# A 256 KB store of zeros on the ACT queue, beside the first loads of a fused multiply and GELU

## The chip, the cores and the metric

One core of a Trainium2 chip runs the kernel alone. The metric is the device time of one execution in microseconds (us), median of several runs.

## The reference

```python
# x, y: 1024 x 4096 float32
z = x * y
return 0.5 * z * (1 + tanh(sqrt(2 / pi) * (z + 0.044715 * z ** 3)))
```

Two inputs of 16.8 MB are read and one output of 16.8 MB is written: 50.33 MB.

## The kernel before

Each of the 128 partitions holds 32768 elements of x in SBUF. They are overwritten in place by the product and then by its GELU. The y values come in three pieces through a ring of half that size. SP issues all loads and stores, and the first two of them stand ahead of the program's first barrier ("hoisted").

```python
X_LOADS = [(0, 16384), (16384, 32768)]
Y_LOADS = [(0, 16384, 0), (16384, 24576, 0), (24576, 32768, 8192)]
STEP = 4096
STORES = [(0, 16384), (16384, 32768)]
# ...
_hoist(nc, [load_x(0).ins, load_y(0).ins])
load_x(1)
for i in (1, 2):
    nc.sync.wait_ge(sem_mul, (Y_LOADS[i][1] - Y_LOADS[1][0]) // STEP)
    load_y(i)

n = 0
for i, (a, b, r) in enumerate(Y_LOADS):
    # ... DVE waits for the x load and the y load concerned
    for c in range(a, b, STEP):
        nc.vector.tensor_mul(out=xs[:, c : c + STEP], in0=xs[:, c : c + STEP],
                             in1=ys[:, r + c - a : r + c - a + STEP]).then_inc(sem_mul, 1)
        n += 1
        nc.scalar.wait_ge(sem_mul, n)
        nc.scalar.activation(out=xs[:, c : c + STEP], in_=xs[:, c : c + STEP],
                             func=GELU).then_inc(sem_act, 1)

for i, (a, b) in enumerate(STORES):
    nc.sync.wait_ge(sem_act, b // STEP)
    nc.sync.dma_start(out=out_r[:, a:b], in_=xs[:, a:b]).then_inc(sem_o[i], 16)
# ... SP waits for both stores
```

So the one SP queue carries, in this order: x (8.4 MB), y (8.4 MB), x (8.4 MB), y (4.2 MB), y (4.2 MB), a store (8.4 MB), a store (8.4 MB).

Of the kernel before, what the change touches and what calls it, by code (L numbers as in the profile page):

```python
# [1 line left out]

# [4 lines left out]


F32 = mybir.dt.float32
GELU = mybir.ActivationFunctionType.Gelu_apprx_tanh  # L10
# [7 lines that stand above are left out]
Y_RING = 16384  # L18


def _hoist(nc, issued):

    here = nc.cur_bb.bb.instructions
    first = nc.main_func.blocks[0].instructions
    for ins in issued:
        del here[next(k for k, i in enumerate(here) if i is ins or i.name == ins.name)]
    engine = issued[0].engine
    at = next(
        k
        for k, i in enumerate(first)  # L30
        if i.engine == engine and type(i).__name__ == "InstDrain"
    )
    first[at:at] = issued


@with_exitstack
def kernel(
    ctx: ExitStack,
    tc: tile.TileContext,
    x: bass.AP,  # L40
    y: bass.AP,
    out: bass.AP,
):
    nc = tc.nc
    P = nc.NUM_PARTITIONS

    x_r = x.flatten_outer_dims().rearrange("(p a) c -> p (a c)", p=P)
    y_r = y.flatten_outer_dims().rearrange("(p a) c -> p (a c)", p=P)
    out_r = out.flatten_outer_dims().rearrange("(p a) c -> p (a c)", p=P)
    total_f = x_r.shape[1]  # L50


    tc.close()
    tc.compile()  # L54

    xs = nc.alloc_sbuf_tensor("xs", [P, total_f], F32).ap()
    ys = nc.alloc_sbuf_tensor("ys", [P, Y_RING], F32).ap()
    sem_x = [nc.alloc_semaphore(f"sem_x{i}") for i in range(len(X_LOADS))]
    sem_y = [nc.alloc_semaphore(f"sem_y{i}") for i in range(len(Y_LOADS))]
    sem_o = [nc.alloc_semaphore(f"sem_o{i}") for i in range(len(STORES))]  # L60
    sem_mul = nc.alloc_semaphore("sem_mul")
    sem_act = nc.alloc_semaphore("sem_act")

    def load_x(i):
        a, b = X_LOADS[i]
        return nc.sync.dma_start(out=xs[:, a:b], in_=x_r[:, a:b]).then_inc(sem_x[i], 16)  # L66

    def load_y(i):
        a, b, r = Y_LOADS[i]
        return nc.sync.dma_start(  # L70
            out=ys[:, r : r + b - a], in_=y_r[:, a:b]
        ).then_inc(sem_y[i], 16)

    _hoist(nc, [load_x(0).ins, load_y(0).ins])
    load_x(1)
    for i in (1, 2):
        nc.sync.wait_ge(sem_mul, (Y_LOADS[i][1] - Y_LOADS[1][0]) // STEP)
        load_y(i)

    n = 0  # L80
    for i, (a, b, r) in enumerate(Y_LOADS):
        for j, (xa, xb) in enumerate(X_LOADS):
            if xa <= a < xb:
                nc.vector.wait_ge(sem_x[j], 16)
        nc.vector.wait_ge(sem_y[i], 16)  # L85
        for c in range(a, b, STEP):
            nc.vector.tensor_mul(  # L87
                out=xs[:, c : c + STEP],
                in0=xs[:, c : c + STEP],
                in1=ys[:, r + c - a : r + c - a + STEP],  # L90
            ).then_inc(sem_mul, 1)
            n += 1
            nc.scalar.wait_ge(sem_mul, n)
            nc.scalar.activation(  # L94
                out=xs[:, c : c + STEP], in_=xs[:, c : c + STEP], func=GELU
            ).then_inc(sem_act, 1)

    for i, (a, b) in enumerate(STORES):
        nc.sync.wait_ge(sem_act, b // STEP)
        nc.sync.dma_start(out=out_r[:, a:b], in_=xs[:, a:b]).then_inc(sem_o[i], 16)  # L100
    for i in range(len(STORES)):
        nc.sync.wait_ge(sem_o[i], 16)
    nums = sorted(s.num for s in [*sem_x, *sem_y, *sem_o, sem_mul, sem_act])
    assert nums == list(range(nums[0], nums[-1] + 1))
    nc.sync.sem_clear(range(nums[0], nums[-1] + 1))


# [1 line left out]
_INS = ['x', 'y']  # L109
_OUTS = [((1024, 4096), 'float32')]  # L110


# [23 lines left out]
```

## Time and profile before

| what | value |
|---|---|
| time, median of 3 runs | 121.02 us (120.82 to 121.17) |
| span of the profiled run | 119.5 us |
| DVE, ACT busy | 29%, 25% |
| packets of the one DMA queue, share of 16 engines | 98.5% |
| bytes read and written | 33.55 + 16.78 MB |

A "packet" in the profile is one record of a transfer on one of the 16 DMA engines. Here each one with data has the size of one partition's row: 64 KB, or 32 KB for the two short y pieces. The records don't name the engine; they were strung together by their times. In the trace of before they string into 16 rows of 63 packets (56 with data), which run side by side: the first packet of each starts between 1.01 and 1.70 us, and together they fill 98.5% of 16 times the span. So a delay of "0.7 us per engine" on all 16 is 0.7 us of the kernel.

These are the two lines of the timeline in which DVE starts on the second and on the third y piece (start, duration, instruction, idle time before and what ended it):

```profile
70.47 8.76 DVE L87 TENSOR_TENSOR xs<-xs,ys 128x4096 f32<-128x4096 f32 x2 [11.70 <-DMA ys<-in_y_dram]
...
80.88 8.76 DVE L87 TENSOR_TENSOR xs<-xs,ys 128x4096 f32<-128x4096 f32 x2 [1.66 <-DMA ys<-in_y_dram]
```

DVE starts 0.09 us after the third piece has landed (80.79 and 80.88 us in the chain of waits), and as soon after the second, so the third landed 10.41 us after the second. For 4.19 MB at the rate of the other stretches (432 to 435 GB/s, worked out in the prediction) 9.7 us would do.

### The profile page before, as it was taken

To read this page: it belongs to the slowest core of one execution; us is meant where nothing else is said; L and a number is where in the kernel's file an instruction comes from. 1 tells how busy PE (TensorE), PEld (TensorE's weight loads), DVE (VectorE), ACT (ScalarE), POOL (GpSimd) and SP (SyncE) were. 2 spreads that over 40 slices of the span, in tenths; PEclk is the share of its full clock that TensorE was granted. 3 is DMA by queue.
4 is the path that set the end of the run, shared out by engine and by line. 5 is a ranking of instruction groups with operands and counts; after the bars stand their busy time and mean duration, and the time that the engine had idled before them with its cause. 6 is when DMAs were issued, how large, how long until landed. Compare 5 with 4: busy or idle time off the path is not lost.

```text
span 119.5 us, 68 instructions
## 1 busy us (share of the span) xinstructions
DVE 35.0 (29%) x8; ACT 30.2 (25%) x9; POOL 0.2 (0%) x4
## 2 busy tenths in 40 slices
DVE  0000000000000199999600049959990000000000
ACT  3000000000000006797780000977479200000000
POOL 0000000000000000000000000000000000000000
DMA  9889888998899889988898989998899888988890
GB/s 351 351 373 680 351 351 351 636 417 351 351 636 417 351 351 526 526 351 351 351 526 351 504 373 482 395 526 351 351 395 658 351 351 351 702 351 351 351 680 22
DMA packets 1008, 50.33 MB, mean 421 GB/s; under 512 B 112, under 2 KB 112, under 8 KB 112
## 3 DMA queue, kind: packets, MB, share of 16 engines
q1 hardware_dynamic: 1008, 50.33, 98.5%
HBM read 33.55 MB, written 16.78 MB: 421 GB/s over the span
## 4 chain that ended last, share of the span: by engine, by line
DMA 53%; DVE 22%; ACT 3%; SPq 0%; issue 0%; DVEq 0%
DMA ys<-in_y_dram 53%; DVE xs L87 22%; ACT xs L94 3%; SPq L66 0%; DVEq L85 0%
## 5 line engine op out<-in xcount | busy, mean ns | idle before, releaser
L87 DVE TENSOR_TENSOR xs<-xs,ys 128x4096 f32<-128x4096 f32 x8 | 35.0, 4421 | 54.7 <-DMA ys<-in_y_dram 54.7
L94 ACT ACTIVATE xs<-xs 128x4096 f32<-128x4096 f32 x8 | 28.9, 3617 | 61.1 <-DVE xs L87 61.1
L94 ACT ACT_TABLE_LOAD x1 | 1.3, 1283 | 1.9 <-PEq L54 1.9
L120 POOL MEMSET const-bfloat16-1.0<- 128x1 bf16 x1 | 0.1, 102 | 0.0
L120 POOL MEMSET const-uint8-127<- 128x1 uint8 x1 | 0.1, 102 | 0.0
L120 POOL MEMSET const-float32-1.0<- 128x1 f32 x1 | 0.1, 99 | 0.0
L120 POOL MEMSET const-float32-0.0<- 128x1 f32 x1 | 0.1, 98 | 0.2 <-issue 0.2
## 6 DMA issues: line engine op xcount, KB each, us to landing
ys<-in_y_dram SPq DMA_DIRECT2D x2, 4096.0 KB, 21.1
xs<-in_x_dram SPq DMA_DIRECT2D x2, 40.3
out_dram<-xs SPq DMA_DIRECT2D x2, 31.9
ys<-in_y_dram SPq DMA_DIRECT2D x1, 40.8
```

What stands on the lines that cost most here:

```text
L87: nc.vector.tensor_mul(out=xs[:, c : c + STEP], in0=xs[:, c : c + STEP], in1=ys[:, r + c - a : r + c - a + STEP],).then_inc(sem_mul, 1)
L94: nc.scalar.activation(out=xs[:, c : c + STEP], in_=xs[:, c : c + STEP], func=GELU).then_inc(sem_act, 1)
L120: nc = _bacc.Bacc("TRN2", target_bir_lowering=False, num_devices=1)
```

## The change

Its intent can be read from the name of the scratch tensor, "first_write": let some harmless write to DRAM be the first one of the execution. DVE fills a small tile with zeros. ACT stores it, each row four times, to a scratch tensor that nobody reads. Both stand ahead of the first barrier. The counts of the multiply semaphore shift by one, because the memset uses the same semaphore.

```diff
+    ws = nc.alloc_sbuf_tensor("ws", [P, 128], F32).ap()
+    sem_w = nc.alloc_semaphore("sem_w")
...
+    scratch = nc.dram_tensor("first_write", [P, 4, 128], F32, kind="Internal").ap()
+    fill = nc.vector.memset(ws[:, :], 0.0).then_inc(sem_mul, 1)
+    ready = nc.scalar.wait_ge(sem_mul, 1)
+    first = nc.scalar.dma_start(out=scratch, in_=ws.unsqueeze(1).to_broadcast([P, 4, 128]))
+    first.then_inc(sem_w, 16)
+    _hoist(nc, [fill.ins])
+    _hoist(nc, [ready.ins, first.ins])
     _hoist(nc, [load_x(0).ins, load_y(0).ins])
...
-        nc.sync.wait_ge(sem_mul, (Y_LOADS[i][1] - Y_LOADS[1][0]) // STEP)
+        nc.sync.wait_ge(sem_mul, 1 + (Y_LOADS[i][1] - Y_LOADS[1][0]) // STEP)
...
-    n = 0
+    n = 1
...
+    nc.sync.wait_ge(sem_w, 16)      # at the end, beside the waits for the stores
```

More of the change, by code (lines that the diff above doesn't have):

```diff
@@ L102 @@
         nc.sync.wait_ge(sem_o[i], 16)
-    nums = sorted(s.num for s in [*sem_x, *sem_y, *sem_o, sem_mul, sem_act])
+    nc.sync.wait_ge(sem_w, 16)
+    nums = sorted(s.num for s in [*sem_x, *sem_y, *sem_o, sem_w, sem_mul, sem_act])
     assert nums == list(range(nums[0], nums[-1] + 1))
```

## The prediction

> **What bounds the kernel now.** I read the page from the top: busy shares, the slices with the DMA row, the queue's share, then the chain of waits.
>
> ```profile
> span 119.5 us, 68 instructions
> DVE 35.0 (29%) x8; ACT 30.2 (25%) x9; POOL 0.2 (0%) x4
> ...
> DMA packets 1008, 50.33 MB, mean 421 GB/s; under 512 B 112, under 2 KB 112, under 8 KB 112
> ...
> q1 hardware_dynamic: 1008, 50.33, 98.5%
> ```
>
> No compute engine is busy for a third of the span, while the packets of the one DMA queue took 98.5% of what 16 engines have. The queue carries 50.33 MB in 112 tiny packets (seven DMAs times 16 engines: the semaphore writes) and 896 large ones. The trace's packet records give the durations: a 64 KB packet takes 2.42 us, a 32 KB one 1.21 us, nearly all alike. Each engine moves 50.33 MB / 16 = 3.146 MB, the equal of 48 packets of 64 KB, so 48 x 2.42 = 116.2 us of the 119.5 are plain transfer.
>
> The chain of waits in order of time seems to tell another story:
>
> ```profile
> 0.44 40.80 DMA ys<-in_y_dram
> ...
> 41.34 17.44 DVE xs L87 x4
> 58.78 0.02 issue
> 58.80 21.99 DMA ys<-in_y_dram
> ...
> 80.88 8.77 DVE xs L87 x2
> ...
> 89.68 3.62 ACT xs L94
> ```
>
> It runs through four multiplications and ends at 93.3 us with the last activation; the last store then takes until 119.4. This is a chain of dependences, not of resources: behind each piece the DMA queue must also be non-empty. It always is. The y pieces are issued at 50.13 and 58.80, while the second x load lands only near 60; the first store is issued at 62.45, when two y pieces are still queued (the second lands at 80.8); the second store is issued at 93.3, and the first lands at 62.45 + 37.7 = 100.15. So the slack of the issues is about 10, 18 and 7 us. What sets the end is the number of bytes and the dead times of the DMA engines.
>
> Where are these dead times? I cut the span at the landings (41.24, 70.40, 80.82, 100.15, end 119.43) and divided the bytes of each piece by its time. The last store has 8.39 MB in 19.28 us, 435 GB/s; the first store 8.39 in 19.33, 434; the second x load with the first y piece 12.58 in 29.13, 432. Two stretches are slower. The first two loads, 16.78 MB, need 38.6 us at 435 GB/s and land at 41.24: 2.7 us of start, of which 1.0 is the time until the first packet and some 0.65 the first packet of each engine (2.6 to 3.3 us instead of 2.42). And the last y piece takes 10.42 us for 4.19 MB, 402 GB/s, where 9.7 would do: 0.7 us lost. In the packet records its last two packets per engine take about 1.8 and 1.35 us instead of 1.21, and they are those just before the first store to HBM. No such loss comes before the second store, nor between any two loads. So the first write to HBM of the execution costs about 0.7 us of all engines' time. This is what the change can aim at: a small early store would pay that cost at a time when the engines wait for their first data anyway.
>
> [...]
>
> **The change part by part.**
>
> 1. A memset of 128 x 128 on DVE before the first barrier. DVE is otherwise idle until 41.3 us. By width, against the 4421 ns of a 4096-wide multiplication, it is some 0.15 to 0.3 us (my estimate). It lies beside the issue of the first loads, on another engine: 0 on the path.
>
> 2. ACT waits for it and issues the store; such an issue keeps a sequencer 0.33 to 0.43 us here. So ACT would reach the first barrier at about 0.3 + 0.4 = 0.7 to 1.0 us, and SP itself gets there only at about 0.9, after its two issues. The barriers may move by some 0.2 us, and with them only the issue of the second x load (1.93 us, needed by the engines at 40) and the activation table load (1.28 us, needed at 45.8). Off the path: 0. The first load is issued at 0.00 by SP and needs nothing from DVE or ACT.
>
> 3. The store's bytes: 262,144 B / 16 = 16 KB for each engine; at 64 KB in 2.42 us, 0.60 us. This is on the path, since the engines have no idle time later.
>
> 4. Its packets. The source repeats a row of 512 B four times, so I expect 512 packets of 512 B, 32 for each engine (or 128 of 2 KB if the written side counts). A pure 512 B is 19 ns; a 4 B packet takes 9 ns in this trace, so 9 ns is a guess for the fixed part of one: 32 x 9 = 0.29 us more. Sum of 3 and 4: about 0.9 us. [...]
>
> 5. What it gives back. If the 0.7 us is a cost of the first write alone, it vanishes at 77 us and is paid by the early store, at 1 to 4 us, where each engine loses 0.65 us anyway. I give this about an even chance; so -0.35 in the mean. In addition some of the store's own work may fall into the 0.65 us in which the engines wait for the first data: perhaps -0.2 in the mean.
>
> 6. The last wait, for the store's semaphore, is long satisfied: one more semaphore instruction at the end, some 0.05 us. The shift of the waits by 1 changes no order.
>
> Sum: 0.6 + 0.29 - 0.35 - 0.2 + 0.05 = +0.4 us. On 121.02 that is 121.4 us.
>
> **The rivals.**
>
> *The warm-up works wholly.* The 0.7 us at 77 us disappears and the early store hides in the start: 0.9 - 0.7 - 0.5, about -0.3, so 120.7. For it: the loss occurs once and before the first store only. Against it: the store reads and writes other addresses than the real one, and if the loss belongs to the output tensor's own addresses, nothing is warmed. Also the engines' turn from loads to stores would still be there if that is the cause.
>
> *Nothing is warmed and all is paid.* The loss at 77 us stays, and the early store adds 0.9 and maybe another 0.7 at the start: +0.9 to +1.6, so 121.9 to 122.6. For it: the engines are full from 1 us to the end, so that whatever one ring takes, the other lacks.
>
> *Bad interleaving.* [...] Against it: between the semaphore packets and the large ones of the present trace there is no visible gap. I give it a few per cent.
>
> *A gain by a second queue.* It would need an engine rate above 27.1 GB/s (64 KB in 2.42 us), and all the large packets sit at that rate. Faster by 2% means 118.6 us or less, thus 2.4 us saved; but all dead time (1.0 until the first packet, 0.65, 0.7, about 0.4 from the last packet to the wait's end) is 2.75 us, and 0.6 us of new bytes are added. Practically impossible.
>
> **The range and the chances.** The three plausible outcomes lie at 120.7, about 121.4 and 121.9 to 122.6; the three runs of before spread by 0.35 us. I take 120.7 to 122.3. Slower by 2% (over 123.4 us) needs short packets costing four times what they should[...]: 4%. Faster by 2%: 1%.
>
> **What would show it right or wrong.** In the changed profile I expect a second hardware queue with 0.26 MB and a share of some 0.5 to 1.5% of the 16 engines; packets under 2 KB up by about 528 if they are of 512 B; the first y landing 0.3 to 1.2 us later than 41.24; every later issue and landing shifted by the same amount, less up to 0.7 us from the last y piece on, if the warm-up works: its landing must then come 9.7 us after the one before it, instead of 10.4. If that distance stays 10.4, the warm-up fell. If the end moves by more than the first y landing, the small packets were spread over the span and cost more than I gave them. An issue of x or of a y piece that arrives after the engines ran empty would show as a gap in the packet records, and would make my whole argument (bytes plus dead times) wrong.

The sum: it came to +0.4 us, thus 121.4 us, in a range from 120.7 to 122.3. Its five terms are estimates from the trace of before. The 0.6 is 16 KB at the rate of a 64 KB packet (2.42 us). The 0.29 takes the 9 ns of a 4 B packet, beside the 19 ns that 512 B need at that rate. The -0.35 is half of the 0.7 us lost at the last y piece, and the -0.2 a part of the 0.65 us by which the first packets are longer. The 0.05 can be compared with a semaphore wait of DVE in the chain of waits: 0.02 us, and 0.03 us of issue before it. That the 0.7 us is a cost of the first write, and that the first packets are longer because the engines wait for data, is how the author read that one trace; it shows the times only.

No 64 KB packet of before took less than 2.418 us. That a store on the ACT queue would share the engines was an assumption when it was written. A "ring" in these texts is the queue of one issuing engine: q1 (SP) and q10 (ACT) on the pages.

## The result, and the profile after

The changed kernel took 121.69 us (median of 4 runs, 121.43 to 121.76), against 120.94 us for the kernel before (4 runs). The ratio is 1.0055, with a 95% interval from 1.0033 to 1.0078. Here and below a ratio is the mean time of one kernel's fast runs over the mean of the other's in the same rounds, so it isn't quite the ratio of the medians. In means the change cost 0.67 us. That is well inside 2%, and the measured time lies inside the predicted range.

First the page of the changed kernel: span, packets and queues.

```profile
span 120.3 us, 70 instructions
...
DMA packets 1536, 50.59 MB, mean 421 GB/s; under 512 B 128, under 2 KB 640, under 8 KB 640
...
q1 hardware_dynamic: 1008, 50.33, 97.9%
q10 hardware_dynamic: 528, 0.26, 0.7%
```

There is a second queue with 528 packets. 512 of them carry 512 B each, and 16 are semaphore writes. Together they took 0.7% of the engines. The mean rate is the same as before, 421 GB/s: the queue was full before and is full now.

The part of the page on DMA issues gives the time from issue to landing in its last column. For the new store:

```profile
first_write<-ws ACTq DMA_DIRECT2D x1, 256.0 KB, 69.7
```

256 KB took 69.7 us to land. The packet records of one engine, in a second trace of the changed kernel, show why:

```
 start us   took ns   bytes   queue
   1.001      3402    65536   q1
   4.400      2418    65536   q1
   6.814        27      512   q10
   6.838      2418    65536   q1
   9.252        27      512   q10
   9.275      2418    65536   q1
```

The engine alternates: one packet of the SP queue, one of the ACT queue. The 32 small packets need 32 turns of about 2.4 us (shorter ones near the end, where y's packets of 32 KB take 1.2). The starts also show the real price of a small packet. From 6.814 to 6.838 the engine is held up for 24 ns, not 27, and the large packet holds it for 2.414 us, not 2.418. Consecutive records overlap by about 4 ns.

Now the chain of waits in order of time, the pieces that answer to those of before:

```profile
0.44 41.17 DMA ys<-in_y_dram
...
41.71 17.44 DVE xs L96 x4
59.15 0.02 issue
59.17 22.34 DMA ys<-in_y_dram
...
81.60 8.77 DVE xs L96 x2
...
90.40 3.62 ACT xs L103
```

And the two lines of the timeline at the last y pieces:

```profile
71.47 8.76 DVE L96 TENSOR_TENSOR xs<-xs,ys 128x4096 f32<-128x4096 f32 x2 [12.34 <-DMA ys<-in_y_dram]
...
81.60 8.76 DVE L96 TENSOR_TENSOR xs<-xs,ys 128x4096 f32<-128x4096 f32 x2 [1.37 <-DMA ys<-in_y_dram]
```

The first y landing is 0.37 us later than before. The second y piece starts to be used 1.00 us later and the third only 0.72 us later (80.88 to 81.60). So the delay grows while the small packets run, and then 0.28 us comes back just where the early write was meant to help: the last piece comes 10.13 us after the one before it instead of 10.41. The packet records add up the same way. From this trace of before to this one of after, the last packet ends 0.79 us later, of which these make 0.78:

- 32 small packets at 23.5 ns (the mean over all of them, start to next start): +0.75 us
- first packets of each engine: +0.03
- some large packets between 36 and 60 us that ran a few per cent longer: +0.21
- both y pieces' 32 KB packets: +0.02 and -0.23

Three theories followed from this. The **tax theory**: each small packet holds its engine for 23.5 ns (bytes and a fixed part), all else is chance. The **warm-up theory**: the early write takes over a part of the loss before the first large store, and the 0.28 us is its gift. The **ring-turn theory**: that loss belongs to the turn from loads to a store inside one ring (here: the queue of one issuing engine, SP or ACT), so no early write on another ring can help it.

"Loss" below is worked out from the packet records: for the packets of y's last piece, the time above the usual 1.211 us each, summed and divided by 16 engines. In the first trace of before it is 0.72 us, in the first of after 0.49 us.

### The profile page after: what moved, and what is told of

It is laid out like the page before. It is cut to its first block, busy times and chain, and to the rows that moved or that the text cites. A ratio compares the mean times of both kernels' runs of the same rounds, so it can differ in the third digit from the quotient of the medians.

```text
span 120.3 us, 70 instructions
## 1 busy us (share of the span) xinstructions
DVE 35.1 (29%) x9; ACT 30.2 (25%) x9; POOL 0.2 (0%) x4
## 2 busy tenths in 40 slices
DMA packets 1536, 50.59 MB, mean 421 GB/s; under 512 B 128, under 2 KB 640, under 8 KB 640
## 4 chain that ended last, share of the span: by engine, by line
DMA 53%; DVE 22%; ACT 3%; SPq 0%; issue 0%; DVEq 0%
DMA ys<-in_y_dram 53%; DVE xs L96 22%; ACT xs L103 3%; SPq L68 0%; DVEq L94 0%
## 6 DMA issues: line engine op xcount, KB each, us to landing
first_write<-ws ACTq DMA_DIRECT2D x1, 256.0 KB, 69.7
```

## The experiments

Twelve kernels ran. All were correct. The diffs are against the changed kernel unless told otherwise.

### 1. Both kernels again

No edit. The aim was a second trace of each.

> The kernel before, unchanged, for a second trace: is the 0.71 us that the last y piece loses before the first store the same each time, and do some large packets between 50 and 60 us always run longer (0.14 us per engine in the first trace)? Tax theory (a small packet takes 27 ns of its engine and nothing else changes): 121.0 us, the last y piece lands 10.3 to 10.5 us after the one before it. Warm-up theory (the early store takes over part of that loss): the same here, 10.4.

Measured: 121.00 us, ratio 1.0011 (0.9992 to 1.0031), as it should be. But its loss was 1.04 us instead of 0.72, and the longer packets between 50 and 60 us were nearly gone (0.04 us in the whole run, against 0.18).

> The changed kernel, unchanged, for a second trace. Its first trace has the last y piece 10.1 us after the one before it instead of 10.4, and 0.38 us per engine of longer large packets between 35 and 60 us instead of 0.14. Warm-up theory: the 10.1 comes again (within 0.1). Tax theory: both differences are chance and may come out elsewhere; the 32 x 27 ns = 0.86 us per engine comes again. Both: +0.6 to +0.8 us over the kernel before.

Measured: 121.38 us, ratio 1.0046 (1.0032 to 1.0060), in means +0.56 us; the interval, +0.39 to +0.73 us, ends just below the tax of 0.75. The loss was 0.46 us, near the first trace. The longer large packets, 0.39 us in the first trace, were absent here (0.00). So that term was chance. The loss also moves by chance, by 0.3 us in two traces of one kernel, and two traces of each can't decide on a gift of 0.25.

### 2. A quarter of the packets, and fewer but larger ones

```diff
-    scratch = nc.dram_tensor("first_write", [P, 4, 128], ...)
+    scratch = nc.dram_tensor("first_write", [P, 128], ...)
-    ... in_=ws.unsqueeze(1).to_broadcast([P, 4, 128])
+    ... in_=ws[:, :]
```

> The early store without the fourfold repeat: 64 KB in 128 packets of 512 B, 8 for each engine. Tax theory: 8 x 27 ns = 0.22 us, so +0.2 us over the kernel before, and the last y piece again 10.4 us after the one before it. Warm-up theory: 0.22 paid and about 0.25 given back, 0.0 us, with the last y piece at 10.1.

Measured: 120.99 us, ratio 1.0010 (0.9996 to 1.0024), in means +0.12 us; loss 0.67 us. Eight packets at 23.5 ns are 0.19 us. Within the interval (-0.05 to +0.29 us), the tax theory holds. The warm-up theory's 0.0 can't be told from it by time, but its second mark, the smaller loss, did not show.

```diff
-    ws = nc.alloc_sbuf_tensor("ws", [P, 128], F32).ap()
+    ws = nc.alloc_sbuf_tensor("ws", [P, 512], F32).ap()
-    scratch = nc.dram_tensor("first_write", [P, 4, 128], ...)
+    scratch = nc.dram_tensor("first_write", [P, 512], ...)
-    ... in_=ws.unsqueeze(1).to_broadcast([P, 4, 128])
+    ... in_=ws[:, :]
```

> The same 256 KB in 128 packets of 2 KB, from a row of 2 KB of zeros, 8 packets for each engine. If a packet costs its bytes at 27.1 B/ns and some 8 ns more, one takes 84 ns and the eight 0.67 us: some 0.2 us less than the changed kernel, so +0.5 us over the kernel before (+0.3 if a warm-up gives back 0.25). If the number of turns between the two rings cost something by itself, it would be cheaper still, since there are 8 turns instead of 32.

Measured: 121.54 us, ratio 1.0053 (1.0039 to 1.0066), in means +0.65 us; loss 0.87 us. The store is issued the same way, yet lands much sooner, because it needs 8 turns and not 32 (page of this run, DMA issues):

```profile
first_write<-ws ACTq DMA_DIRECT2D x1, 256.0 KB, 24.1
```

By the starts in the records, a 2 KB packet holds its engine for 80 ns: 8 x 80 = 0.64 us. That gives two equations: 80 - 23.5 = 56.5 ns for 1536 B is 27.2 B/ns, and 512 B / 27.2 = 18.8 ns leaves 4.7 ns of fixed cost for a packet, if it is the same for both sizes. It seems to be: the same two numbers give 607, 1209 and 2414 ns for 16, 32 and 64 KB, and these are the usual distances of starts in the records. So a 512 B packet moved at 80% of the rate of its bytes alone (18.8 of 23.5 ns), a 2 KB packet at 94% (75.3 of 80). The bytes (0.60 us) are most of the price. The repeat of a 512 B row costs only some 0.1 us more than 2 KB rows.

### 3. Four times the packets

```diff
-    scratch = nc.dram_tensor("first_write", [P, 4, 128], ...)
+    scratch = nc.dram_tensor("first_write", [P, 16, 128], ...)
-    ... to_broadcast([P, 4, 128])
+    ... to_broadcast([P, 16, 128])
```

> The early store four times as long: 1 MB in 2048 packets of 512 B, 128 for each engine. By the starts of consecutive packets in the traces so far, a 512 B packet delays its engine by 23.6 ns (its bytes 18.9, and 4.7 more). Tax theory: 128 x 23.6 ns = 3.0 us, so +2.9 to +3.1 us, four times the change, whatever the loss before the first large store (0.45 to 1.03 us in the traces so far) happens to be. If turns between rings had a cost of their own that the big packets hide, or if the early store gave something back that does not grow with it, the slope would differ: e.g. +3.3 for 0.3 us given back once in the changed kernel. Since there are fewer large packets left than small ones, the store may land only at the end.

Measured: 123.80 us, ratio 1.0237 (1.0217 to 1.0257), in means +2.89 us; the loss was 0.76 us. The price grows with the packets: 128 x 23.5 ns = 3.01 us. This interval (2.6 to 3.1 us) contains it, and excludes the 3.3 us that the expectation named for a gift of 0.3 us in the changed kernel. That 3.3 took the price of a packet from the times. With the price read from the records, a single gift of 0.3 us would give 2.7 us, which the interval doesn't exclude. The page shows the store landing after all else, though it was issued first:

```profile
q10 hardware_dynamic: 2064, 1.05, 2.8%
...
first_write<-ws ACTq DMA_DIRECT2D x1, 1024.0 KB, 122.0
```

In the records, some 67 small packets of each engine were left when the last large one ended. They ran back to back for 1.6 us, again about 23.5 ns each. With the queue of large packets gone, the same tax is simply paid in one piece.

### 4. The same transfer in other places

**A load instead of the store.**

```diff
+    wl = nc.alloc_sbuf_tensor("wl", [P, 4, 160], F32).ap()
-    ... out=scratch, in_=ws.unsqueeze(1).to_broadcast([P, 4, 128])
+    ... out=wl[:, :, 0:128], in_=x_r[:, 0:512].rearrange("p (a b) -> p a b", a=4)
```

> A load in the place of the store: 256 KB of x in 512 packets of 512 B into a spare tile, on the ACT queue at the same time; the memset stays. Tax theory: as dear as the store, 32 packets per engine at about 27 ns, +0.6 to +0.9 us; the last y piece 10.1 to 10.4 us after the one before it, as in the changed kernel. Warm-up theory: no write comes early, so the last y piece is again at 10.4 while the changed kernel has 10.1.

Measured: 121.38 us, ratio 1.0048 (1.0032 to 1.0065), in means +0.55 us; the loss was 0.75 us. So the direction of the small transfer makes no difference to the time that these runs can see.

**The store issued late.** Here the store is taken from the start and stands behind ACT's sixth activation in ACT's program. The trace shows the issue at 79.24 us, as that activation begins, and the first small packets from 83.3 us on.

```diff
-    ready = nc.scalar.wait_ge(sem_mul, 1)
-    first = nc.scalar.dma_start(...)   # at the start
...
+            if n == 7:
+                first = nc.scalar.dma_start(out=scratch, in_=ws.unsqueeze(1).to_broadcast([P, 4, 128]))
+                first.then_inc(sem_w, 16)
```

> The same store of 256 KB in 512 B packets, but issued by ACT after its sixth activation, near 83 us, beside the large stores. Tax theory: the same 32 x 23.6 ns = 0.76 us, so +0.5 to +0.8 us, with all y landings as in the kernel before. Warm-up theory: nothing early, so the whole tax without anything given back, +0.76, and the changed kernel is better than this by 0.2 or more.

Measured: 121.79 us, ratio 1.0064 (1.0049 to 1.0080), in means +0.81 us; loss 1.12 us. The tax of 0.75 us is there without anything early. It looks slightly dearer than the early store (0.56 to 0.70 us in the runs that have it), but the intervals of the two overlap: 0.59 to 0.97 us here, and 0.39 to 0.73 us for the changed kernel in its second series.

**The store first, alone.** SP does not issue the first load until the store has landed.

```diff
-    _hoist(nc, [load_x(0).ins, load_y(0).ins])
+    landed = nc.sync.wait_ge(sem_w, 16)
+    _hoist(nc, [landed.ins, load_x(0).ins, load_y(0).ins])
```

> SP waits for the landing of the early store before it issues the first load, so that the first write is over before anything else moves. The span grows by the store's whole latency, which this measures[...]. Warm-up theory: the loss before the first large store vanishes (last y piece 9.7 us after the one before it, not 10.4). Tax theory: it stays at 10.1 to 10.4.

Measured: 123.80 us, ratio 1.0242 (1.0229 to 1.0255), in means +2.90 us. The page and the chain of waits:

```profile
first_write<-ws ACTq DMA_DIRECT2D x1, 256.0 KB, 2.6
...
61.54 22.12 DMA ys<-in_y_dram
```

With the engines to itself, the store lands 2.6 us after its issue, not 69.7. The first load starts at 2.84 us, and the end moves by about that. Above all, the first write of the execution is over here, with certainty, before anything else moves, and still the loss before the first large store is 0.93 us. A first write of this size warms nothing that could be seen.

**The store into the output tensor.** It goes to 512 columns of the output, and the real store waits for it.

```diff
-    scratch = nc.dram_tensor("first_write", [P, 4, 128], F32, kind="Internal").ap()
+    scratch = out_r[:, 0:512].rearrange("p (a b) -> p a b", a=4)
...
+    nc.sync.wait_ge(sem_w, 16)          # ahead of the stores, in place of the wait at the end
```

> The early store goes to the first 512 columns of the output itself instead of a scratch tensor (the real store overwrites it later and waits for it; that wait ends near 70 us and the queue is busy until 80). If the loss at 77 us is a first touch of the output tensor's addresses, it vanishes: last y piece at 9.7, +0.2 us over the kernel before. If not, it is as the changed kernel: +0.6 to +0.8, last y piece at 10.1 to 10.4.

Measured: 121.55 us, ratio 1.0060 (1.0048 to 1.0072), in means +0.70 us; loss 0.78 us. Each row's first 2 KB of the first output half had been written before. So the loss isn't a first touch of these rows either, as far as 2 KB of each can show it.

### 5. What the loss belongs to

**The small store inside the SP ring**, between y's first load and x's second:

```diff
-    ready = nc.scalar.wait_ge(sem_mul, 1)
-    first = nc.scalar.dma_start(...)
+    nc.sync.wait_ge(sem_mul, 1)
+    first = nc.sync.dma_start(out=scratch, in_=ws.unsqueeze(1).to_broadcast([P, 4, 128]))
     load_x(1)
...                                     # the lines that hoist the first loads move up
```

> The same early store on the SP queue behind the first two loads, so that its packets stand in one block of the one ring, between y's first load and x's second. If the 0.7 us belongs to every turn from loads to a store inside a ring, it is lost just before this block too (near 40 us) and again at 77: +0.86 + 0.7 = +1.6 us. If it belongs to the first write of the execution, it is lost near 40 us and not at 77 (last y piece 9.7 us after the one before it): +0.9 us. If small stores don't cause it at all: +0.86, with 10.4 at the last y piece.

Measured: 121.27 us, ratio 1.0034 (1.0022 to 1.0046), in means +0.39 us. Just before the small store the large packets lost only some 0.05 us; at y's last piece the loss was 0.63. So neither form of "every turn" or "first write" holds for a small store. The price is below the 0.75 us that the 32 packets still cost by their records (23.5 ns each, back to back), and the interval, +0.27 to +0.56 us, excludes it. The one profiled run, itself the slowest of the five, doesn't show where some 0.36 us of it went. That stays open.

**A large store inside the SP ring**, 2 MB in packets of 16 KB from a piece of x, at the same place:

```diff
-    scratch = nc.dram_tensor("first_write", [P, 4, 128], ...)
+    scratch = nc.dram_tensor("first_write", [P, 4096], ...)
...                                     # the wait and the issue on ACT are taken out
+    nc.sync.wait_ge(sem_x[0], 16)
+    first = nc.sync.dma_start(out=scratch, in_=xs[:, 12288:16384])
     load_x(1)
...
+            if c == 12288:
+                nc.vector.wait_ge(sem_w, 16)     # DVE overwrites that piece only after it was stored
```

> A larger early store inside the one ring: 2 MB in 128 packets of 16 KB from a piece of x, behind the first two loads and before x's second. Bytes and packets: 8 x (602 + 5) ns = 4.86 us. If the loss of 0.45 to 1.03 us belongs to every turn from loads to a store of large packets inside a ring, it appears twice, just before this block (near 39 us) and again before the first real store (near 82): +5.5 to +5.9 us. If it belongs to the first large store of the execution, it appears near 39 alone: +4.8. If it belongs to that place alone (the real store's), near 82 alone: +4.8.

Measured: 126.33 us, ratio 1.0445 (1.0418 to 1.0471), in means +5.40 us, of which 4.86 are the bytes and packets. In the packet records of one engine, the loss now stands ahead of this store and is gone ahead of the real one:

```
 start us   took ns   bytes
  35.514      2420    65536    y, first load
  37.931      3751    65536    y, first load, its last packet: 1.33 us too long
  41.678         9        4
  41.683       611    16384    the early store
  ...
  82.647      1218    32768    y, last piece
  83.861      1249    32768    y, last piece, its last packet
  85.107         9        4
  85.113      2418    65536    the real store
```

Over all engines, the loss was about 0.95 us ahead of the early store, and 0.14 us ahead of the real one; in no other trace was the latter below 0.46. The chain of waits shows the first of the two as a later landing:

```profile
0.43 41.66 DMA ys<-in_y_dram
```

against 40.80 in the kernel before, although nothing had been added to the queue ahead of that landing. DVE and ACT were idle at that time, so the loss isn't due to their work either. The idea of the change, that the first store pays something once, is thus supported by this one trace, but only for a large store. The bytes of such a store cost far more than the loss. About 0.3 us of the +5.40 stays unexplained: the profiled run was the fastest of the four.

**The first real store on the ACT queue.** This diff is against the kernel before:

```diff
             ).then_inc(sem_act, 1)
+            if n == 5:
+                a0, b0 = STORES[0]
+                nc.scalar.wait_ge(sem_act, b0 // STEP)
+                nc.scalar.dma_start(out=out_r[:, a0:b0], in_=xs[:, a0:b0]).then_inc(sem_o[0], 16)
...
     for i, (a, b) in enumerate(STORES):
+        if i == 0:
+            continue
```

> The kernel before, without any early store, but the first large store is issued on the ACT queue after the fifth activation (near 78.5 us), so that it does not stand behind y's last piece in the same ring. If the loss belongs to the turn from loads to a store inside a ring, most of the 0.7 us vanishes: -0.4 to -0.8 us against the kernel before. If it belongs to the beginning of the store wherever it stands, no change: 120.8 to 121.1 us. y's last piece may land up to 2.4 us later, which the slack of 7 us of the second store's issue covers.

Measured: 120.97 us, ratio 0.9994 (0.9978 to 1.0009), no change. The store stands in a ring of its own (page, DMA queues):

```profile
q1 hardware_dynamic: 864, 41.94, 82.3%
q10 hardware_dynamic: 144, 8.39, 16.2%
```

and the loss is 0.64 us, as ever. So the ring-turn theory falls: the loss comes ahead of the first large store, in whichever ring it stands.

The test separates less than it was meant to. The timeline has the issue as the fifth activation begins, not after it:

```profile
74.86 0.37 ACTq L100 DMA_DIRECT2D out_dram<-xs  x1
```

Yet the first packet of this store starts only at 79.72 us, and on each of the 16 engines it follows y's last data packet, as in the kernel before. The long packets are again the last two y packets of each engine. So this run doesn't tell "first large store" from "any turn of an engine from loads to a large store" or "the end of y's last piece". Only the trace of the large store above speaks against these two: the real store follows y's last piece there too, with a loss of 0.14.

This was also the only candidate for a version better than both, and it isn't one.

### The runs together

Means are differences of the mean times of the same rounds. The tax is packets per engine x 23.5 ns (80 ns for 2 KB, 607 ns for 16 KB).

| kernel | added packets per engine | tax, us | measured mean, us | loss in the trace, us |
|---|---|---|---|---|
| before, two traces | 0 | 0 | 0 and +0.14 | 0.72, 1.04 |
| changed, two series | 32 x 512 B | 0.75 | +0.67, +0.56 | 0.49, 0.46 |
| quarter | 8 x 512 B | 0.19 | +0.12 | 0.67 |
| 2 KB packets | 8 x 2 KB | 0.64 | +0.65 | 0.87 |
| fourfold | 128 x 512 B | 3.01 | +2.89 | 0.76 |
| into the output | 32 x 512 B | 0.75 | +0.70 | 0.78 |
| inside the SP ring | 32 x 512 B | 0.75 | +0.39 | 0.63 |
| alone, ahead of all | waits 2.84 us | | +2.90 | 0.93 |
| load instead | 32 x 512 B | 0.75 | +0.55 | 0.75 |
| late | 32 x 512 B | 0.75 | +0.81 | 1.12 |
| large, inside the ring | 8 x 16 KB | 4.86 | +5.40 | 0.14 |
| real store on ACT | 0 | 0 | -0.07 | 0.64 |

The mean loss of the five traces without an early write (before twice, load, late, real store on ACT) is 0.85 us. That of the eight with an early small write (changed twice, quarter, 2 KB, fourfold, output, ring, alone) is 0.70. Both groups spread by several tenths and overlap, though the two lowest of these losses are those of the changed kernel itself. A gift of some 0.15 us isn't excluded, and would bring tax and time closer together, but it isn't shown.

## Why the prediction was right

The time and the chief mechanism were right. One step of the sum was wrong (a gift of 0.55 us) and another mis-sized (0.14 us too dear). The second made up for only a quarter of the first, so the sum of +0.4 us lies 0.2 to 0.3 us under the measured means. That the time fell into the range is no support for the gift: without it, the prediction's own sum is +0.94, thus 121.96 us, and that lies in the range of 120.7 to 122.3 too.

- **What bounds the kernel** (bytes plus dead times of full DMA engines; the chain through DVE and ACT has slack): right. The added packets cost their tax and no more, at one, four and a quarter times the size; only inside the SP ring they cost 0.36 us less than that, which stays open. In the late kernel the tax was paid at another time and cost about the same.
- **Steps 1 and 2** (memset and issue off the path): right. The memset took 165 ns, inside the estimate. The issue on ACT took 0.55 us, more than the 0.33 to 0.43 of SP's issues. The issue of x's second load moved from 1.93 to 2.24 us in both traces, which nobody waited for. (That the early issue on ACT moves it isn't shown: in the traces of the quarter, the load and the store into the output it stayed at 1.91 or 1.92.)
- **Step 3** (bytes, 0.60 us): right. 27.2 B/ns is what the two packet sizes give.
- **Step 4** (fixed cost of a small packet): the size was off. The packets were the expected 512 of 512 B, but the fixed part was guessed as 9 ns from the duration of a 4 B packet. Durations in the records overlap with the next packet by about 4 ns, and the starts give 4.7 ns. The sum of steps 3 and 4 is 0.75 us (32 x 23.5 ns), not 0.89.
- **Step 5** (a gift of 0.35 + 0.2 us in the mean): failed. That the 0.7 us is "a cost of the first write alone", which any early store would pay, fell with the store that ran alone first: 0.93 us was lost all the same. That a part of the store would be done while the engines wait for their first data fell with the packet records: in the second trace of the changed kernel the engine shown has its first small packet at 6.8 us, after two large ones, and thereafter one for each turn (in neither trace does any small packet start before 6.5 us); the first packets' loss did not shrink (0.71 and 0.67 us per engine before, 0.74 and 0.86 after).
- **Step 6** (0.05 us for the last wait): nothing to be seen. From the end of the last packet to the end of the span it is 0.46 us before and 0.45 after.
- **Rivals.** "Nothing is warmed and all is paid" is what came, with 0.75 in place of 0.9 to 1.6. The mark given for it, a distance of 10.4 at the last y piece, did not show in the changed kernel (10.13); the loss behind this mark moves by some tenths, between two traces of one kernel and among kernels with the same tax, so one trace couldn't decide by it. "Bad interleaving" was right about the pattern, one small packet at each turn, and wrong about the price: a change of ring has none that shows, since small packets cost 23.5 ns in turns (changed kernel) and back to back (the end of the fourfold one).
- The last mark of the prediction was read badly: "if the end moves by more than the first y landing", the small packets would cost more than expected. The end did move by more (0.8 us against 0.37), and the packets were spread over 70 us, but they cost less.

What stays open: what it is, ahead of the first large store, that costs 0.46 to 1.12 us per engine in thirteen of the fourteen traces (in the fourteenth, some 0.95 us ahead of the 2 MB store that came before it), and what it takes to pay it earlier (bytes, packet size or the kind of source); 2 MB in packets of 16 KB did in one trace, 256 KB in packets of 512 B or 2 KB did not.

## What to carry to other kernels

Here the DMA engines were full from start to end (98.5%), and on the ACT queue beside SP's transfers, early or late, added bytes cost about their time however idle ACT was: +0.12 to +2.89 us measured, where the packets make 0.19 to 3.01. (Inside the SP ring 256 KB cost less, +0.39 where the packets make 0.75.) In such a kernel, take the bytes per engine over the measured rate (27.2 B/ns here) and the fixed cost for each packet (4.7 ns here) before hoping for a gift. In these traces a transfer on a second queue beside long packets got one packet per turn, so give it few large packets if anybody waits for it (24.1 us instead of 69.7 to land here for the same 256 KB). And before a bubble of half a microsecond in one trace is called a cause, take a second trace of the same kernel: this one moved by 0.3 us by itself.
